# S5 + pooling + short-convolution trunk: ScalarE empties the small PSUM tiles of the S5 input part, and the recurrence's VectorE operations are spread one by one

## Chip, cores and metric

One core of a Trainium2 chip. The metric is the device time of one launch in microseconds (us). The kernel before took 1664.32 us as the median of three runs (1661.87 to 1665.4).

## What is computed

A trunk of two layers on x of 1 x 1024 x 1024 in float32. The part that matters here is branch A of the first layer, a diagonal complex state-space mixer (S5) with 64 groups of 16 channels and 64 complex states each:

```python
h = rmsnorm(h_res, norm_g[layer])
u_a, g_a, u_b, g_b = split(h @ ev_w_in, 4)
# s5_mixer, per group g:
dt = exp(log_dt);  lb = exp(lam * dt)            # complex
bb = ((lb - 1) / lam) * b                        # complex
bu = einsum('blgh,gph->blgp', u_a, bb)
s  = associative_scan(s[t] = lb * s[t-1] + bu[t])
y  = real(einsum('blgp,ghp->blgh', s, c)) + d_skip * u_a
y  = gelu(y);  z = y @ w_glu + b_glu;  y_a = val * sigmoid(gate)
# branch B: causal pooling over windows 2, 4, 8, 16, then small matmuls
h_res += concat([y_a * silu(g_a), y_b * silu(g_b)]) @ ev_w_out
```

The second layer (short gated convolution) and a last rmsnorm follow.

## The kernel before

**Matmuls.** Every large product is a list of units, run in order on TensorE (PE). A unit of `mm_full` is 8 blocks over the contraction dimension (k-blocks); each is six matmuls of 128x512 (weights split into `whi` + `wlo`, activations into `a` + `t`, three products, two column halves; L114). The accumulators `acc` are a ring of 3 PSUM tiles. The units are: 0 to 7 "ua" (input of S5), 8 and 9 "ga" 0 and 1 (gate of S5), 10 to 29 four groups of "ub", "ub", "gb", "gb", "pool" (branch B), 30 to 35 "ga" 2 to 7, 36 to 43 "fb" (output projection of B), then the GLU, "fa", the second layer and its output. For each unit its weights are split (ScalarE makes `whi`, L81; VectorE `wlo`, L82), and `evac_*` empties `acc` (a VectorE operation 128x1024 first).

**The written order.** All engines take their instructions in program order. Work that isn't a unit's own stands in three tables by unit: `pre`, `post`, and `mids`. `mm_full` puts a unit's list of `mids` into the seven gaps between its k-blocks (`spread`). The small matmuls among them write `aux`, a ring of 2 PSUM tiles: a third small product waits until the first tile has been emptied.

**S5 input part (units 6 to 9).** POOL (GpSimd) prepares tables (`s5_tables`, to about 85 us), then for each k of 0 to 7 a tile Z(k) (`z_build`: a product on VectorE or POOL, 128x896, and further products and sums on POOL). `t_work(k)`: three pieces; each multiplies Z(k) by identity columns and by C1 (L390) into `aux`; from there 128 columns per group go to the tile M (ScalarE, L391) and 16 to the tile K (VectorE adds them to what is in K, a diagonal of skip weights that POOL put there). `x_work(k)`: two pieces; M times the layer's input U (L408) into `aux`, and from there to W (tile name `big`): the first 64 partitions by ScalarE (L416), the others by VectorE (L414).

```python
        o = [lambda k=k: s5_step(k // 2 - 1, True)] if k in (2, 4, 6) else []
        at_mid(s, [t[0], x[0], t[1], x[1], *n, t[2], *b, *o])
    at_mid(9, [*x_work(7), lambda: s5_step(3, True)])
    for i, m in enumerate((("gb", 7), ("ga", 2), ("ga", 3), ("ga", 4))):
        at_mid(idx[m], [lambda i=i: s5_step(i, False)])
```

**Recurrence.** The states stand in W as 128 chunk values (NC) for each of 32 pairs of groups. `s5_step(i, odd)` adds to the odd (or even) columns of one quarter of W the products of their left neighbours with lambda: four VectorE operations on 128x1024 (even: 128x1008), product, add, product, add, with the scratch tile `t9`. Between the odd and the even steps `s5_scan` on POOL runs over the odd columns (63 rounds of four small operations, after unit 9). `s5_kd` stores K in DRAM through a zeroed tile in `t9` (ahead of unit 10).

**Output of the state part.** `y_prep(k)` (POOL, ScalarE) prepares, and the two pieces of `y_work(k)` (units ga3 to ga6 and fb1 to fb4) multiply into `aux` (L485, L486) and apply gelu in five operations: ScalarE square (L487), VectorE multiply-add (L236), VectorE product with `aux` (L230), ScalarE tanh (L490), VectorE sum and product (L491), which is the last to read `aux`.

**Ahead of unit 0's end.** ScalarE computes sines for the tables (L299 to L301, behind POOL), then loads another function table and takes the square root for the first rmsnorm (L154); VectorE makes `rs` from it and PE spreads `rs` over the partitions (L168).

Of the kernel before, what the change touches and what calls it, by code (L numbers as in the profile page):

```python
# [8 lines left out]
F32 = mybir.dt.float32  # L9
# [5 lines left out]
P = 128  # L15
# [3 lines left out]
NG = 64  # L19
# [8 lines left out]
def trunk(ctx: ExitStack, tc: tile.TileContext, a: dict, out: bass.AP):  # L28
# [177 lines left out]
    limW = cp.tile([P, 2, 32], F32, name="limW")  # L206
    lre2 = cp.tile([P, 32], F32, name="lre2")
    lim2 = cp.tile([P, 2, 32], F32, name="lim2")
    st1 = cp.tile([P, 2, 32], F32, name="st1")
    st2 = cp.tile([P, 2, 32], F32, name="st2")  # L210
    fri = cp.tile([P, 2, NG], F32, name="fri")

    s5 = {}
# [15 lines left out]
    def tt(e, o, x, y, op):  # L229
        e.tensor_tensor(out=o, in0=x, in1=y, op=op)  # L230
# [48 lines left out]
    def s5_tables():  # L279
# [45 lines left out]
        for i in range(2):  # L325
# [3 lines left out]
            e.tensor_copy(cols_of(limW[p0, 1]), by[p0, 1, :, i])  # L329

        tt(e, lre2, lreW, lreW, ALU.mult)
        tt(e, st1[:, 0], limW[:, 0], limW[:, 0], ALU.mult)
        tt(e, lre2, lre2, st1[:, 0], ALU.subtract)
        both = lambda x: x.unsqueeze(1).to_broadcast([P, 2, 32])
        tt(e, lim2, limW, both(lreW), ALU.mult)
        ts(e, lim2, lim2, 2.0, ALU.mult)

        s5["K"] = slot("K", [P, NG, NH])
        tt(e, s5["K"], mask.unsqueeze(1).to_broadcast([P, NG, NH]),
           w[:, 3].unsqueeze(2).to_broadcast([P, NG, NH]), ALU.mult)  # L340
        ts(e, s5["C1"], s5["C1"], sgn[:, 0:1], ALU.mult)

    def s5_b():
        P1, P2 = s5["P1"], s5["P2"]
# [36 lines left out]
    def t_work(k):  # L381

        def piece(g0, g1):
            if g0 == 0:
                s5["M", k] = slot(("t1", "t6")[k % 2], [P, 8, P])
            n = g1 - g0
            ps = aux_tile()
            v = ps[:, : IW * n].rearrange("p (g x) -> p g x", x=IW)
            for g in range(g0, g1):
                PE.matmul(v[:, g - g0], lhsT=s5["Z", k][:, g], rhs=s5["IC"][k % 2][:, g], start=True, stop=True)  # L390
            A.activation(s5["M", k][:, g0:g1], v[:, :, 0:P], AF.Copy)  # L391
            kk = s5["K"][:, 8 * k + g0 : 8 * k + g1]
            tt(V, kk, kk, v[:, :, P:], ALU.add)

        return [lambda: piece(0, 3), lambda: piece(3, 6), lambda: piece(6, 8)]

# [5 lines left out]
    def x_work(k):  # L402
        def piece(q):
            W, U = s5["W"], s5["U"][k]
            ps = aux_tile()
            for i in range(4):
                g = 4 * q + i
                PE.matmul(ps[:, i * P : i * P + P], lhsT=s5["M", k][:, g], rhs=U[:, g], start=True, stop=True)  # L408
            p0 = slice(64 * (k % 2), 64 * (k % 2) + 64)
            g0 = (k // 2) * 8 + 4 * q  # L410
            for ri in range(2):
                o = W[p0, ri, g0 : g0 + 4].rearrange("p a b -> p (a b)")
                if ri:
                    V.tensor_copy(o, ps[64:128])  # L414
                else:
                    A.activation(o, ps[0:64], AF.Copy)  # L416

        return [lambda: piece(0), lambda: piece(1)]

# [9 lines left out]

    def s5_step(i, odd):  # L430

        W, gs = s5["W"], slice(8 * i, 8 * i + 8)
        n = NC // 2 if odd else NC // 2 - 1
        src = W[:, :, gs, 0:NC:2] if odd else W[:, :, gs, 1 : NC - 1 : 2]
        dst = W[:, :, gs, 1:NC:2] if odd else W[:, :, gs, 2:NC:2]
        t = slot("t9", [P, 2, 8, NC // 2])[:, :, :, 0:n]
        sh = [P, 2, 8, n]
        re, im = lreW[:, gs].unsqueeze(1).unsqueeze(3).to_broadcast(sh), limW[:, :, gs].unsqueeze(3).to_broadcast(sh)
        for x, f in ((src, re), (src[:, ::-1], im)):
            tt(V, t, x, f, ALU.mult)  # L440
            tt(V, dst, dst, t, ALU.add)

    def s5_scan():
        W = s5["W"]
        re = lre2.unsqueeze(1).to_broadcast([P, 2, 32])
        for c in range(3, NC, 2):
            tt(G, st1, W[:, :, :, c - 2], re, ALU.mult)
            tt(G, st2, W[:, ::-1, :, c - 2], lim2, ALU.mult)
# [26 lines left out]
    def y_work(k):  # L475
        def piece(q):
# [577 lines left out]
    for k in range(8):  # L1054
# [2 lines left out]
        t, x = t_work(k), x_work(k - 1) if k else [lambda: None] * 2  # L1057
        b = [lambda k=k: z_build(k + 2)] if k < 6 else []
        n = [lambda k=k: u_load(k + 1, UT[(k + 1) % 2])] if k < 7 else []
        o = [lambda k=k: s5_step(k // 2 - 1, True)] if k in (2, 4, 6) else []  # L1060
        at_mid(s, [t[0], x[0], t[1], x[1], *n, t[2], *b, *o])
    at_mid(9, [*x_work(7), lambda: s5_step(3, True)])
    for i, m in enumerate((("gb", 7), ("ga", 2), ("ga", 3), ("ga", 4))):
        at_mid(idx[m], [lambda i=i: s5_step(i, False)])
    at(pre, 10, s5_kd)
    at(post, 9, s5_scan)

    def c2_load():
        s5["C2"] = slot("C2", [P, NG, NH])
# [391 lines left out]
```

## Time and profile before

| | |
|---|---|
| median of three runs | 1664.32 us (1661.87 to 1665.4) |
| the profiled execution | 1662.76 us, its span in the trace 1661.0 us |
| busy: PE / VectorE (DVE) / ScalarE (ACT) / GpSimd (POOL) | 96% / 67% / 32% / 40% of the span |
| mean granted TensorE clock | 0.978 |

Times of the trace are counted from the span's start. PE is the engine that sets the end; a gap on it, or a stretch in which its clock was granted at half, is time lost.

### The profile page before, as it was taken

Reading aid. Unit: us, or ns where it says so; the run is one execution under the profiler, and the core shown is the slowest. Engines: PE = TensorE matmul, PEld = TensorE weight load, DVE = VectorE, ACT = ScalarE, POOL = GpSimd, SP = SyncE. Lnnn points to the kernel's source line nnn. Section 1 sums busy time; section 2 is a strip of 40 time slices with the busy share of each in tenths; the row PEclk is TensorE's granted clock in tenths of the full one; section 3 lists DMA queues with packets and bytes.
Section 4 is the critical chain, followed back from the end, with each engine's and each line's share of the span. In section 5 each row is a group of like instructions: output and inputs, shape, how many; then the busy total and the mean of one; then the engine's idle time right before and its main releaser. Section 6 shows DMA issues by size and latency. Waiting matters only on the chain.

```text
span 1661.0 us, 19044 instructions
## 1 busy us (share of the span) xinstructions
PE 1594.5 (96%) x7186; PEld 1318.9 (79%) x7186; DVE 1107.8 (67%) x1302; ACT 537.7 (32%) x777; POOL 664.4 (40%) x638
## 2 busy tenths in 40 slices
PE   9987999999799999999969999999999999999997
PEld 8776888888688878888747888888888888878886
DVE  5546646679765686672599776868686877763544
ACT  6132211112353343341433332323333233343531
POOL 6962399806312443201264534535343435300001
PEclk9998999999899999999989999999999999999998
DMA  5232362123486722224402212221221212156353
GB/s 210 102 102 76 85 174 91 50 70 127 139 292 201 255 90 76 77 79 149 151 1 76 77 51 76 66 87 52 76 77 57 96 51 77 55 199 207 123 149 117
DMA packets 95034, 181.29 MB, mean 109 GB/s; under 512 B 16352, under 2 KB 52960, under 8 KB 94432
## 3 DMA queue, kind: packets, MB, share of 16 engines
q10 hardware_dynamic: 49664, 116.41, 21.7%
q1 hardware_dynamic: 45280, 63.68, 11.4%
q8 instruction: 57, 0.93, 0.2%
q14 instruction: 33, 0.27, 0.1%
HBM read 141.33 MB, written 42.93 MB: 111 GB/s over the span
## 4 chain that ended last, share of the span: by engine, by line
PE 58%; DVE 5%; issue 1%; DMA 1%; ACT 0%; ACTq 0%; DVEq 0%
PE acc L682 43%; PE acc L929 9%; PE acc L114 4%; PE acc L833 1%; DVE t L230 1%; DVE a L82 1%; DVE a L85 1%; DVE ws L82 1%; PE acc L972 1%; DMA t<-in_glu 0%; DMA hpd<-t 0%; PE aux L168 0%; DVE big L82 0%; ACTq L907 0%; PE aux L150 0%
## 5 line engine op out<-in xcount | busy, mean ns | idle before, releaser
L682 PE MATMUL acc<-a,ws 128*128 128x512 f32 x1920 | 450.5, 390 | 5.5 <-DVE t L230 2.4
L682 PEld LDWEIGHTS acc<-a,ws 128*128 128x128 f32 x1920 | 361.1, 188 | 82.9 <-ACT a L81 3.8
L114 PE MATMUL acc<-a,whi 128*128 128x512 f32 x1440 | 396.6, 398 | 0.1
L114 PEld LDWEIGHTS acc<-a,whi 128*128 128x128 f32 x1440 | 271.5, 191 | 55.7 <-issue 0.9
L230 POOL TENSOR_TENSOR t<-t,t 128x512 f32<-128x512 f32 (+2 forms) x81 | 147.7, 1823 | 308.4 <-DVE ws L82 183.7
L682 PE MATMUL acc<-big,ws 128*128 128x512 f32 x960 | 230.1, 395 | 11.5 <-DVE big L82 4.1
L82 DVE TENSOR_TENSOR wlo<-raw,whi 128x1024 fp32r<-128x1024 f32 (+2 forms) x89 | 114.5, 1289 | 188.3 <-ACT whi L81 188.1
L81 ACT ACTIVATE ws<-t 128x512 fp32r<-128x512 f32 x200 | 125.8, 630 | 338.1 <-PE acc L682 205.5
L682 PEld LDWEIGHTS acc<-big,ws 128*128 128x128 f32 x960 | 182.1, 190 | 53.1 <-DVE big L82 5.4
L114 PE MATMUL acc<-a,wlo 128*128 128x512 f32 x720 | 223.9, 392 | 0.0
L82 DVE TENSOR_TENSOR ws<-t,ws 128x512 fp32r<-128x512 f32 x200 | 182.5, 913 | 33.4 <-ACT ws L81 31.6
L114 PEld LDWEIGHTS acc<-a,wlo 128*128 128x128 f32 x720 | 136.7, 190 | 29.0
L929 PE MATMUL acc<-a,whi 128*128 128x512 f32 x480 | 150.3, 394 | 1.5 <-ACT a L84 1.1
L81 ACT ACTIVATE whi<-raw 128x1024 fp32r<-128x1024 f32 (+2 forms) x89 | 86.8, 978 | 198.1 <-PE acc L114 128.4
L230 DVE TENSOR_TENSOR t<-t,acc 128x512 f32<-128x512 f32 x134 | 91.1, 681 | 50.6 <-PE acc L682 50.5
L682 PE MATMUL acc<-td,ws 128*128 128x512 f32 x480 | 117.3, 393 | 1.3 <-DVE td L82 1.3
L682 PEld LDWEIGHTS acc<-td,ws 128*128 128x128 f32 x480 | 90.6, 189 | 21.9 <-DVE td L82 1.7
L929 PEld LDWEIGHTS acc<-a,whi 128*128 128x128 f32 x480 | 90.7, 189 | 21.7 <-ACT a L84 1.5
L230 POOL TENSOR_TENSOR t<-C,LR 128x1024 f32<-128x1024 f32 (+1 forms) x18 | 40.1, 2231 | 160.5 <-PE aux L486 70.7
L929 PE MATMUL acc<-a,wlo 128*128 128x512 f32 x240 | 94.3, 393 | 0.0
L230 POOL TENSOR_TENSOR t<-t,rs 128x512 f32<-128x512 f32 x5 | 8.7, 1746 | 198.4 <-ACT rs L169 198.4
L230 POOL TENSOR_TENSOR raw<-raw,raw 128x512 f32<-128x512 f32 x20 | 26.7, 1336 | 120.6 <-DVE ws L82 120.6
(259 smaller groups left out, 1986.8 us busy)
## 6 DMA issues: line engine op xcount, KB each, us to landing
raw<-in_scin ACTq DMA_DIRECT2D x32, 512.0 KB, 4.1
t<-in_scin ACTq DMA_DIRECT2D x32, 512.0 KB, 4.3
raw<-in_scout ACTq DMA_DIRECT2D x32, 512.0 KB, 3.7
raw<-in_win ACTq DMA_DIRECT2D x29, 512.0 KB, 3.6
t<-ud ACTq DMA_DIRECT2D x16, 512.0 KB, 4.0
raw<-in_wout ACTq DMA_DIRECT2D x16, 512.0 KB, 3.7
big<-y2d ACTq DMA_DIRECT2D x15, 512.0 KB, 6.1
ud<-t SPq DMA_DIRECT2D x8, 512.0 KB, 2.6
```

The costliest lines, as they stand in the source:

```text
L81: A.activation(h, src, AF.Copy)
L82: (e or V).tensor_tensor(out=l, in0=src, in1=h, op=ALU.subtract)
L85: V.scalar_tensor_tensor(out=l, in0=src, scalar=scale, in1=h, op0=ALU.mult, op1=ALU.subtract)
L114: PE.matmul(acc[:, n * 512 : n * 512 + 512], lhsT=w, rhs=x[:, n * 512 : n * 512 + 512], start=first and i == 0, stop=last and i == 2)
L230: e.tensor_tensor(out=o, in0=x, in1=y, op=op)
L682: PE.matmul(bank, lhsT=wt, rhs=x[:, k], start=k == 0 and j == 0, stop=k == 3 and j == 2)
L833: PE.matmul(u.acc[:, hs], lhsT=w, rhs=x[:, hs], start=k == 0 and j == 0, stop=k == NK - 1 and j == 2)
L929: PE.matmul(acc[:, 0:512], lhsT=w, rhs=x[:, n % 2], start=n == 0 and i == 0, stop=n == 15 and i == 2)
L972: PE.matmul(acc, lhsT=wt, rhs=x[:, n % 2, quarter(q)], start=n == 0 and i == 0, stop=n == 15 and i == 2)
```

## The change

- `t_work`: K gets its 16 columns by a ScalarE copy, no longer by a VectorE add. POOL no longer fills K with the skip diagonal; instead the new `s5_skip`, after unit 9, makes the diagonal in `t9` and adds it to K (two VectorE operations on 128x1024).
- The sign that C1 is multiplied by (128x1024) is applied by ScalarE, no longer by POOL.
- `x_work`: both halves of W by ScalarE.
- `s5_step` returns its four operations singly; the odd ones stand between the pieces of `t_work` and `x_work`, over two k's, the last odd step moves to unit 10. The even steps stand one unit earlier each (gb6, gb7, ga2, ga3), spread singly. `s5_scan` moves behind unit 10.
- gelu: the square takes its factor as the ScalarE operation's scale; one VectorE operation (`(w + 1) * aux`) stands for two.
- Scratch tiles st1, st2 are replaced by other scratch.

```diff
         tt(e, lre2, lreW, lreW, ALU.mult)
-        tt(e, st1[:, 0], limW[:, 0], limW[:, 0], ALU.mult)
-        tt(e, lre2, lre2, st1[:, 0], ALU.subtract)
+        tt(e, tm[:, 0:32], limW[:, 0], limW[:, 0], ALU.mult)
+        tt(e, lre2, lre2, tm[:, 0:32], ALU.subtract)
...
-        tt(e, s5["K"], mask.unsqueeze(1).to_broadcast([P, NG, NH]),
-           w[:, 3].unsqueeze(2).to_broadcast([P, NG, NH]), ALU.mult)
-        ts(e, s5["C1"], s5["C1"], sgn[:, 0:1], ALU.mult)
+        V.tensor_copy(skip, w[:, 3])
+        A.activation(s5["C1"], s5["C1"], AF.Copy, scale=sgn[:, 0:1])
+
+    def s5_skip():
+
+        t = slot("t9", [P, NG, NH])
+        tt(V, t, mask.unsqueeze(1).to_broadcast([P, NG, NH]), skip.unsqueeze(2).to_broadcast([P, NG, NH]), ALU.mult)
+        tt(V, s5["K"], s5["K"], t, ALU.add)
...
             A.activation(s5["M", k][:, g0:g1], v[:, :, 0:P], AF.Copy)
-            kk = s5["K"][:, 8 * k + g0 : 8 * k + g1]
-            tt(V, kk, kk, v[:, :, P:], ALU.add)
+            A.activation(s5["K"][:, 8 * k + g0 : 8 * k + g1], v[:, :, P:], AF.Copy)
...
-                if ri:
-                    V.tensor_copy(o, ps[64:128])
-                else:
-                    A.activation(o, ps[0:64], AF.Copy)
+                A.activation(o, ps[64 * ri : 64 * ri + 64], AF.Copy)
...
-        for x, f in ((src, re), (src[:, ::-1], im)):
-            tt(V, t, x, f, ALU.mult)
-            tt(V, dst, dst, t, ALU.add)
+        def product(x, f, first):
+            if first:
+                tmp["t"] = slot("t9", [P, 2, 8, NC // 2])[:, :, :, 0:n]
+            tt(V, tmp["t"], x, f, ALU.mult)
+
+        take = lambda: tt(V, dst, dst, tmp["t"], ALU.add)
+        return [lambda: product(src, re, True), take, lambda: product(src[:, ::-1], im, False), take]
...
-            A.activation(w, ps, AF.Square)
-            ts(V, w, w, 0.044715, ALU.mult, 1.0, ALU.add)
-            tt(V, w, w, ps, ALU.mult)
+            A.activation(w, ps, AF.Square, scale=math.sqrt(0.044715))
+            V.scalar_tensor_tensor(out=w, in0=w, scalar=1.0, in1=ps, op0=ALU.add, op1=ALU.mult)
...
-        o = [lambda k=k: s5_step(k // 2 - 1, True)] if k in (2, 4, 6) else []
-        at_mid(s, [t[0], x[0], t[1], x[1], *n, t[2], *b, *o])
-    at_mid(9, [*x_work(7), lambda: s5_step(3, True)])
-    for i, m in enumerate((("gb", 7), ("ga", 2), ("ga", 3), ("ga", 4))):
-        at_mid(idx[m], [lambda i=i: s5_step(i, False)])
+        if k % 2 == 0:
+            o = [lambda k=k, i=i: odd_work[k // 2 - 1][i]() for i in range(4)] if k else [lambda: None] * 4
+            at_mid(s, [t[0], x[0], t[1], x[1], *n, o[0], t[2], *b])
+        else:
+            at_mid(s, [t[0], o[1], x[0], t[1], o[2], x[1], *n, t[2], o[3], *b])
+    at_mid(9, x_work(7))
+    at_mid(10, [lambda i=i: odd_work[3][i]() for i in range(4)])
+    for i, m in enumerate((("gb", 6), ("gb", 7), ("ga", 2), ("ga", 3))):
+        at_mid(idx[m], [lambda i=i, j=j: even_work[i][j]() for j in range(4)])
+    at(post, 9, s5_skip)
     at(pre, 10, s5_kd)
-    at(post, 9, s5_scan)
+    at(post, 10, s5_scan)
```

Where the instructions stand. In these rows `big` is W, `t<-B,LR` a product of `z_build`, and numbers behind a name tell buffers apart.

First place: VectorE in unit 7, before. The first row empties `aux` of the last t piece of k = 2.

```order
L230 TENSOR_TENSOR K_409<-K_409,aux_979 128x32
L230 TENSOR_TENSOR t_98_990<-B_50_657,LR_142 128x128x7
L230 TENSOR_TENSOR t_100_997<-big_804,lreW 128x1024
L230 TENSOR_TENSOR big_804<-big_804,t_100_997 128x2x512
L230 TENSOR_TENSOR t_100_997<-big_804,limW 128x1024
L230 TENSOR_TENSOR big_804<-big_804,t_100_997 128x2x512
L230 TENSOR_TENSOR K_409<-K_409,aux_1009 128x48
L414 COPY big_804<-aux_1015 64x512
L230 TENSOR_TENSOR K_409<-K_409,aux_1028 128x48
```

All four operations of the odd step stand together, and behind them the K add and the W copy of the pieces of k = 3. After the change, VectorE in the same unit:

```order
L229 TENSOR_TENSOR t_97_978<-big_803,lreW 128x1024
L229 TENSOR_TENSOR t_99_991<-B_50_656,LR_143 128x128x7
L229 TENSOR_TENSOR big_803<-big_803,t_97_978 128x2x512
L229 TENSOR_TENSOR t_97_978<-big_803,limW 128x1024
L229 TENSOR_TENSOR big_803<-big_803,t_97_978 128x2x512
L229 TENSOR_TENSOR t_108_1053<-B_50_656,LR_143 128x128x7
L82 TENSOR_TENSOR wlo_1067<-raw_925,whi_1066 128x1024
```

The VectorE has no operation on `aux` left there, and its next split of weights stands behind the step. What empties `aux` is ScalarE; its rows in the second half of unit 7 after the change (`aux_999` and `aux_1019` are t pieces of k = 3, `aux_1012` and `aux_1032` x pieces; x2: both halves):

```order
L394 ACTIVATE t_101_998<-aux_999 128x384
L395 ACTIVATE K_408<-aux_999 128x48
L415 ACTIVATE big_803<-aux_1012 64x512 x2
L394 ACTIVATE t_101_998<-aux_1019 128x384
L395 ACTIVATE K_408<-aux_1019 128x48
L415 ACTIVATE big_803<-aux_1032 64x512 x2
```

The copy of `aux_1012` writes W behind the step's first add, that of `aux_1032` behind its second product (both by data).

Second place: VectorE from unit gb6 to the last pool unit, before. The first row is branch B's split of its pooled input, the `acc` rows are evacuations, L516 the gate's product; `acc_2771` is unit gb7's.

```order
L82 TENSOR_TENSOR td_265_2630<-t_274_2705,td_264_2629 128x1024
L82 TENSOR_TENSOR wlo_2761<-raw_2686,whi_2760 128x512
L230 TENSOR_TENSOR t_278_2766<-acc_2711,rs_290 128x1024
L516 SCALAR_TENSOR_TENSOR t_278_2766<-t_279_2767,t_278_2766 128x1024
L230 TENSOR_TENSOR t_281_2814<-big_804,lreW 128x16x63
L230 TENSOR_TENSOR big_804<-big_804,t_281_2814 128x2x8x63
L230 TENSOR_TENSOR t_281_2814<-big_804,limW 128x16x63
L230 TENSOR_TENSOR big_804<-big_804,t_281_2814 128x2x8x63
L82 TENSOR_TENSOR wlo_2826<-raw_2764,whi_2825 128x1024
L230 TENSOR_TENSOR t_284_2831<-acc_2771,rs_290 128x1024
L516 SCALAR_TENSOR_TENSOR t_284_2831<-t_285_2832,t_284_2831 128x1024
L82 TENSOR_TENSOR wlo_2863<-raw_2829,whi_2862 128x1024
```

After the change (the first row is the last operation of the even step that now stands in gb6; L520 is the same gate product, `acc_2778` gb7's accumulator):

```order
L229 TENSOR_TENSOR big_803<-big_803,t_277_2726 128x2x8x63
L82 TENSOR_TENSOR wlo_2768<-raw_2688,whi_2767 128x512
L229 TENSOR_TENSOR t_280_2773<-acc_2713,rs_289 128x1024
L520 SCALAR_TENSOR_TENSOR t_280_2773<-t_281_2774,t_280_2773 128x1024
L229 TENSOR_TENSOR t_283_2791<-big_803,lreW 128x16x63
L229 TENSOR_TENSOR big_803<-big_803,t_283_2791 128x2x8x63
L229 TENSOR_TENSOR t_283_2791<-big_803,limW 128x16x63
L229 TENSOR_TENSOR big_803<-big_803,t_283_2791 128x2x8x63
L82 TENSOR_TENSOR wlo_2833<-raw_2771,whi_2832 128x1024
L229 TENSOR_TENSOR t_286_2838<-acc_2778,rs_289 128x1024
L520 SCALAR_TENSOR_TENSOR t_286_2838<-t_287_2839,t_286_2838 128x1024
L82 TENSOR_TENSOR wlo_2870<-raw_2836,whi_2869 128x1024
```

One even step (rows of 128x1008 elements) more stands ahead of the `wlo` that unit ga2 multiplies with and of the operation that empties gb7's accumulator.

Third place: ScalarE between the sines and the square root of the first rmsnorm, before.

```order
L300 ACTIVATE td_11_185<-td_11_185 128x64
L301 ACTIVATE td_11_185<-td_11_185,half_pi 128x64
L154 ACT_TABLE_LOAD
L154 ACTIVATE rsm<-rsm 128x8
L81 ACTIVATE whi_549<-raw_281 128x1024
```

After the change:

```order
L299 ACTIVATE td_11_184<-td_11_184 128x64
L300 ACTIVATE td_11_184<-td_11_184,half_pi 128x64
L338 ACTIVATE C_14_204<-C_14_204,sgn 128x1024
L154 ACT_TABLE_LOAD
L154 ACTIVATE rsm<-rsm 128x8
L81 ACTIVATE whi_548<-raw_280 128x1024
```

The multiplication of C1 by its sign stands between the last sine and the table load for the square root.

## Rows read from the trace of the kernel before

**Rows 1.** Waits of PE from 80 to 190 us: total, times, longest.

```profile
PE aux L390 <- DVE K L230: 12.9, 6, 4.0
```

**Rows 2.** Timeline, PE: start, us, instruction [idle before, and its releaser].

```profile
44.42 3.59 PE L168 MATMUL aux<-rs,ones 128*128 128x512 f32 x4 [2.46 <-DVE rs L230]
...
90.61 1.81 PE L390 MATMUL aux<-td,t 128*128 128x144 f32 x6 [4.47 <-POOL t L230]
...
126.91 1.81 PE L390 MATMUL aux<-td,t 128*128 128x144 f32 x6 [4.04 <-DVE K L230]
...
153.27 1.59 PE L390 MATMUL aux<-td,t 128*128 128x144 f32 x6 [4.02 <-DVE K L230]
...
167.24 1.81 PE L390 MATMUL aux<-td,t 128*128 128x144 f32 x6 [2.75 <-DVE K L230]
...
382.38 1.07 PE L114 MATMUL acc<-a,whi 128*128 128x512 f32 x4
...
383.74 1.07 PE L114 MATMUL acc<-a,whi 128*128 128x512 f32 x4
...
418.59 0.46 PE L485 MATMUL aux<-t,td 128*128 128x128 f32 x2 [3.88 <-issue]
...
438.74 0.77 PE L485 MATMUL aux<-t,td 128*128 128x128 f32 x2 [5.15 <-DVE B L491]
```

**Rows 3.** Stretches: PE, PEld, DVE, ACT, POOL busy (x count), PE clock, DMA share, GB/s.

```profile
89.00:96.00 7.00, 5.39 (x19) 4.82 (x20) 1.10 (x2) 0.49 (x1) 6.89 (x4) 0.54 0.42 164
...
126.00:133.00 7.00, 6.09 (x21) 5.52 (x22) 2.44 (x5) 1.67 (x3) 0.00 (x0) 0.52 0.14 40
...
153.00:157.00 4.00, 3.73 (x16) 3.58 (x17) 1.11 (x4) 1.41 (x3) 0.00 (x0) 0.57 0.00 0
...
436.00:444.00 8.00, 5.26 (x21) 4.95 (x22) 5.91 (x9) 2.83 (x5) 0.00 (x0) 0.57 0.23 66
```

**Rows 4.** Timeline, POOL: end of the tables, and the first operation after the scan.

```profile
81.03 1.94 POOL L230 TENSOR_TENSOR K<-con,td 128x1024 f32<-128x1024 f32 x1
...
82.95 2.86 POOL L234 TENSOR_SCALAR C<-C,sgn 128x1024 f32<-128x1024 f32 x1
...
387.01 2.73 POOL L230 TENSOR_TENSOR t<-C,LR 128x1024 f32<-128x1024 f32 x1 [59.82 <-DVE t L581]
```

**Rows 5.** Timeline, DVE, unit 7.

```profile
119.92 2.87 DVE L230 TENSOR_TENSOR big<-big,t 128x1024 f32<-128x1024 f32 x1
...
122.83 2.64 DVE L230 TENSOR_TENSOR t<-big,limW 128x1024 f32<-128x1024 f32 x1
...
126.65 0.20 DVE L230 TENSOR_TENSOR K<-K,aux 128x48 f32<-128x48 f32 x1
```

**Rows 6.** Lines by shape, 80 to 190 us: busy, mean ns, idle before and releasers.

```profile
L414 DVE COPY big<-aux 64x512 f32<-64x512 f32 x16 | 11.1, 694 | 16.8 <-ACT big L416 16.7
...
L416 ACT ACTIVATE big<-aux 64x512 f32<-64x512 f32 x16 | 9.4, 590 | 27.0 <-DVE big L230 14.2 <-PE aux L408 12.8
```

**Rows 7.** Timeline, ACT: an operation of 128x1024 with a column as scale.

```profile
19.85 1.14 ACT L1265 ACTIVATE a<-big,vec 128x1024 fp32r<-128x1024 f32 x1
```

**Rows 8.** Timeline, DVE, units gb7 to ga4.

```profile
372.93 1.20 DVE L230 TENSOR_TENSOR t<-big,lreW 128x1008 f32<-128x1008 f32 x1
...
377.78 1.23 DVE L82 TENSOR_TENSOR wlo<-raw,whi 128x1024 fp32r<-128x1024 f32 x1
...
378.93 1.22 DVE L230 TENSOR_TENSOR t<-acc,rs 128x1024 f32<-128x1024 f32 x1
...
383.22 1.23 DVE L82 TENSOR_TENSOR wlo<-raw,whi 128x1024 fp32r<-128x1024 f32 x1 [0.66 <-ACT whi L81]
...
403.29 1.91 DVE L230 TENSOR_TENSOR t<-big,lreW 128x1008 f32<-128x1008 f32 x1
...
414.17 2.14 DVE L236 TENSOR_SCALAR K<-K 128x512 f32<-128x512 f32 x1
...
417.80 0.69 DVE L491 SCALAR_TENSOR_TENSOR B<-K,aux 128x512 f32<-128x512 f32 x1 [0.70 <-ACT K L490]
```

More of the change, by code (lines that the diff above doesn't have):

```diff
@@ L200, in trunk @@
     rsm = cp.tile([P, 3, 8], F32, name="rsm")
+    skip = cp.tile([P, NG], F32, name="skip")
     psch = cp.tile([P, 8], F32, name="psch")
@@ L208, in trunk @@
     lim2 = cp.tile([P, 2, 32], F32, name="lim2")
-    st1 = cp.tile([P, 2, 32], F32, name="st1")
-    st2 = cp.tile([P, 2, 32], F32, name="st2")
     fri = cp.tile([P, 2, NG], F32, name="fri")
@@ L435, in s5_step @@
         dst = W[:, :, gs, 1:NC:2] if odd else W[:, :, gs, 2:NC:2]
-        t = slot("t9", [P, 2, 8, NC // 2])[:, :, :, 0:n]
-        sh = [P, 2, 8, n]
+        sh, tmp = [P, 2, 8, n], {}
         re, im = lreW[:, gs].unsqueeze(1).unsqueeze(3).to_broadcast(sh), limW[:, :, gs].unsqueeze(3).to_broadcast(sh)
-        for x, f in ((src, re), (src[:, ::-1], im)):
-            tt(V, t, x, f, ALU.mult)
-            tt(V, dst, dst, t, ALU.add)
+        def product(x, f, first):
[4 more added lines that the diff above has]
+        return [lambda: product(src, re, True), take, lambda: product(src[:, ::-1], im, False), take]
     def s5_scan():
@@ L445, in s5_scan @@
         re = lre2.unsqueeze(1).to_broadcast([P, 2, 32])
+        st1, st2 = (fri[:, i].rearrange("p (r g) -> p r g", r=2) for i in range(2))
         for c in range(3, NC, 2):
@@ L1042, in trunk @@
     s5["U"] = {}
+    odd_work, even_work = [], []
     def w_alloc():
         s5["W"] = slot("big", [P, 2, 32, NC])
+        odd_work.extend(s5_step(i, True) for i in range(4))
+        even_work.extend(s5_step(i, False) for i in range(4))
     def at_mid(s, work):
```

## Prediction

> **What bounds the kernel now.** I read the timeline of TensorE first, for its gaps, since it is busy 96% of the span: what it waits for inside 80 to 450 us is what the change can give back. In the S5 input part it waits six times for the VectorE's K add, 12.9 us in all [rows 1]; the three large ones are 4.04 us at 126.91, 4.02 at 153.27 and 2.75 at 167.24, so the other three make 2.1. Ahead of these it waits 4.47 us at 90.61 for POOL, and in the output part 3.88 us at 418.59 and 5.15 at 438.74 [rows 2]. The releaser of 418.59 is given as "issue", but the tile that this product needs is freed by the gelu's last operation, 417.80 + 0.69 = 418.49 [rows 8], so it is a VectorE wait too.
>
> Then the stretches behind these gaps: the granted clock averages 0.54, 0.52 and 0.57 in them, which is about the lower of the two levels (1.2 of 2.4 GHz), and it fell after a gap of 4 us or more in each case [rows 3]. What a stretch loses is its PE time by (1 - clock): 5.39 x 0.46 = 2.5 us after 90.61, 6.09 x 0.48 = 2.9 after 126.91, 3.73 x 0.43 = 1.6 after 153.27, 5.26 x 0.43 = 2.3 after 438.74.
>
> Last the VectorE's rows, to see why K is late: the odd step's four operations stand in one block. Two of them take 2.87 and 2.64 us, and only then, at 126.65, comes the K add of 0.20 us that TensorE waits for [rows 5].
>
> **First t piece (gain 7.0).** POOL drops the K product (1.94) and the C1 scaling (2.86) that stand just ahead of Z(0) [rows 4]. TensorE's wait ends at 90.61 on a POOL product; moved up by 4.80 us it would come at 85.8, and TensorE arrives at 90.61 - 4.47 = 86.1. So the wait goes, and I count its slow clock as gone too: 4.5 + 2.5. Bounds: 0 if something else is late there (7.0 lost), and no more than 7.0.
>
> **C1 on ScalarE (loss 1.1).** The operation stands between the sines and the table load that precedes the first square root, whose result TensorE waits for at 44.42 (2.46 us) [rows 2]. A ScalarE operation of 128x1024 with a column as scale took 1.14 us [rows 7], and the whole of it is on that chain. Bounds 0 and 1.14 plus a slower stretch; the clock is already low there.
>
> **K and W copies, odd steps (gain 10.4 + 4.5).** After the change nothing of VectorE frees `aux` in units 6 to 9; ScalarE does. The price of a W copy is 590 ns on ScalarE against 694 on VectorE [rows 6]. So two copies in series, 1.18, are no longer than one of each, 1.28. The K copy (128x48 or 128x32) has no row on ScalarE; it lies between nothing and the 0.59 of ten times its columns, and I take 0.2, as the VectorE's add [rows 5].
>
> The Trainium skill, "ScalarE: Activation LUTs", Rules for kernel authors, speaks against such a move: simple elementwise work belongs on VectorE, up to about three times as fast per element in bf16. If that held here, a pair of copies would end some 3 us later and the gaps would stay, about 15 us of the sum. The rows above say the contrary for fp32 out of PSUM.
>
> What ScalarE waits for now is data: the x copy that follows an odd step's first add must wait for that add. In unit 7 the add ran from 119.92 to 122.8 [rows 5]. It now has the Z product between it and the step's first product, which has moved ahead of the piece by which Z is paced; so it may start some 1.2 us earlier, and 0.4 more as the small wait before is gone: about 118.3, end 121.2 if it is as long as before. Two copies take it to 122.4; TensorE comes for the tile at 126.91 - 4.04 - 0.4 = 122.5. That is no margin, but no wait to speak of: I count both 4 us gaps, the three small ones and the slow stretches of 2.9 and 1.6 us as gone. Bounds: 0 to 1.5 us left in each of units 7 and 8.
>
> In unit 9 the wait of 2.75 us stays but for 0.3: ScalarE reaches its M and K copies only behind the tanh of the gate unit 8, which waits for the VectorE's split and evacuation as before. Bounds of its gain: 0 and 2.75 with its slow stretch of 1.6.
>
> So 12.9 - 2.75 + 0.3 = 10.4, and 2.9 + 1.6 = 4.5.
>
> **Last odd step, skip and scan (0).** The step in unit 10 has to wait for the DMA of `s5_kd` that reads the zeroed `t9`, and the scan starts after it, up to 20 us later than before. POOL was idle for 59.82 us ahead of 387.01, so it ended at 327.2 [rows 4]; the even steps need it at 369, so 20 us are covered. If the scan came 42 us later, every further one would be TensorE's. Behind the waiting step on VectorE stands the weight split of two units later: covered unless the DMA takes over 15 us.
>
> **Even steps one unit earlier, gelu (gain 4.0).** VectorE has no free time from gb6 on. A step takes 377.78 - 372.93 = 4.85 us there. One more of them now stands ahead of the `wlo` (377.78) and of the evacuation of gb7's accumulator (378.93, 1.22 us) [rows 8]. The evacuation ends at 378.93 + 4.85 + 1.22 = 385.0. Unit ga2 takes that accumulator at 382.38 [rows 2]: a new wait of 2.6 us. All VectorE work behind it is 4.85 late, less the 0.66 us that it idled at 383.22, so 4.2. The first gelu piece ended at 418.49; it now has one operation less (2.14 us at 414.17) [rows 8], so it ends at 418.5 + 4.2 - 2.1 = 420.6. TensorE waits for it as before, 2.0 us later, and the product stands one k-block (383.74 - 382.38 = 1.36 us) earlier in its unit, with that much left to do: 3.4 lost in all, the ga2 wait inside it, as TensorE is early there. But no step stands in ga4 any more (it ran for 10.9 us in front of the first gelu, 403.29 to 414.17, as one does before 438.74), so the wait there goes: 5.15 + 2.3 - 3.4 = 4.0. The other gelu operations saved lie where VectorE isn't waited for. Bounds: -3.4 (438.74 stays) to 7.4 (nothing new).
>
> **Sum.** 7.0 - 1.1 + 10.4 + 4.5 + 4.0 = 24.8 us. On the profiled execution 1662.76 - 24.8 = 1638.0; the median shown is 1.6 above that execution, so I predict 1639.
>
> **The rivals.**
>
> *ScalarE is held by the steps.* If POOL's Z operations run beside all four operations of an odd step, as in the step from 403.29 to 414.17, which takes 10.9 us instead of 4.85 [rows 8], the adds end 1 to 1.6 us later than I have them, and the x copies, with the M and K copies behind them on ScalarE, free the tiles late: 1.5 us at two or three places in units 7 and 8, with a slow stretch in each: 3 to 9 us. Time 1642 to 1648. For it: no margin in my schedule, and the add and the product in unit 7 already took 2.87 and 2.64. The Trainium skill, "GPSIMD Engine Reference", Specifications, says that GpSimd's SBUF interfaces are shared with VectorE, with contention for VectorE operations with two SBUF inputs. By that rule all four would be slowed whenever POOL works; the trace agrees, as the same shape takes 1.2 us without POOL.
>
> *The VectorE's queue at gb6 to ga3.* The extra 4.85 us costs a slow stretch after the ga2 wait (1.6, as after 153.27) that isn't absorbed, and one more wait at ga5: the 4.0 are lost, with 1 to 3 more. Time 1643 to 1646.
>
> *The gaps only change hands.* Units 7 and 8 wait for ScalarE's copies as long as for VectorE's: 8.1 + 4.5 stay. Time 1652. Against it: the K copies no longer stand behind the block.
>
> *Slower than before.* In units 7 to 9 ScalarE holds everything that frees `aux`, so one late add delays three pieces, not one. Nine pieces late by 3 us each, with a slow clock behind five of them (some 2 us each, as above), cost 27 + 10 = 37 us on top of the forecast, whose units 7 and 8 have no gaps: 1638 + 37 = 1675. It decides where the pieces are late by 1.7 us each, since 9 x 1.7 + 10 is the forecast's 25. Against it: VectorE has several short operations less per unit there.
>
> **Chances.** The forecast, 1633 to 1644: 0.66. ScalarE held: 0.13. VectorE's queue: 0.10. Gaps change hands: 0.04. Better than forecast, by a unit 9 wait that goes and a first root without loss (1628 to 1633): 0.03. Slower: 0.02, and as much for a time within 0.2% of before, which is about what a measurement of this kernel can tell from no change. Faster by more than that: 0.96. The range of 8 in 10 takes the first three: 1631 to 1649.
>
> **What would show it.** Right: no wait at 86, 122 and 149 us, the wait at 44 longer by 1.1, one of 2 to 3 us in unit 9, a new one of about 2.6 at ga2, one of 3 to 5 at ga4, none at ga5. Wrong: waits of L393 on ScalarE's W copies in units 7 and 8, or VectorE waits at ga5 to ga6.

## The result, and the profile after

The changed kernel takes 1636.09 us (median of four runs, 1634.49 to 1639.64) against 1663.87 us before (the three runs shown ahead and a fourth): ratio 0.9837, 95% interval 0.9817 to 0.9857, so 27.8 us less. Forecast were 1639, range 1631 to 1649. The profiled execution took 1635.34 us with a span of 1633.5.

Waits of PE after the change (total, times, longest). Of the six waits for K [rows 1] and the two in the output part, one each is left, the last and the first of these lines; the other two, for unit gb7's accumulator at ga2 (2.6) and for a load (1.5), are new:

```profile
PE aux L490 <- issue: 4.1, 1, 4.1
...
PE acc L114 <- DVE t L229: 2.6, 1, 2.6
...
PE aux L490 <- DMA td<-md: 1.5, 1, 1.5
...
PE aux L393 <- ACT K L395: 1.5, 1, 1.5
```

Where they lie, in PE's timeline after (start, us, instruction, [idle before and releaser]), in answer to [rows 2]:

```profile
46.76 3.65 PE L168 MATMUL aux<-rs,ones 128*128 128x512 f32 x4 [5.01 <-DVE rs L229]
...
88.35 0.90 PE L393 MATMUL aux<-td,t 128*128 128x144 f32 x6
...
116.01 0.90 PE L393 MATMUL aux<-td,t 128*128 128x144 f32 x6
...
134.56 0.90 PE L393 MATMUL aux<-td,t 128*128 128x144 f32 x6
...
146.85 1.00 PE L393 MATMUL aux<-td,t 128*128 128x144 f32 x6 [1.47 <-ACT K L395]
...
361.99 1.17 PE L114 MATMUL acc<-a,whi 128*128 128x512 f32 x4 [2.58 <-DVE t L229]
...
397.22 0.46 PE L490 MATMUL aux<-t,td 128*128 128x128 f32 x2 [4.15 <-issue]
...
415.12 0.46 PE L490 MATMUL aux<-t,td 128*128 128x128 f32 x2 [1.54 <-DMA td<-md]
```

There is no idle time ahead of the first t product (88.35), and none ahead of the second t products of k = 3 (116.01) and k = 5 (134.56), the places of the 4.04 and 4.02 us before. PE runs there at full clock, where it ran at about half of it behind these gaps [rows 3]; two stretches (the clock stands behind the five engines' busy times):

```profile
89.00:96.00 7.00, 7.00 (x41) 6.11 (x40) 3.90 (x3) 2.71 (x10) 4.67 (x3) 1.00 0.48 165
...
126.00:133.00 7.00, 7.00 (x44) 6.23 (x43) 3.90 (x4) 3.83 (x12) 1.97 (x2) 1.00 0.46 152
```

A slow stretch stays in the output part: behind the 4.15 us at 397.22 the granted clock averages 0.66 from 397 to 402 us.

To say where the time came from, I cut the span of both traces at instructions that both have: the first rms product (L168), the first and last t product (L390, after: L393), the first and last output product (L486, after: L491) and the last input matmul (L114). Each number is the difference of two starts in one trace, in us; differences named below are taken before rounding:

| | to first rms | to first t | t part | to first output | output part | to last L114 | rest | span |
|---|---|---|---|---|---|---|---|---|
| before | 44.4 | 46.2 | 91.2 | 218.4 | 142.7 | 257.2 | 860.9 | 1661.0 |
| after | 46.8 | 41.6 | 70.4 | 222.7 | 135.6 | 256.9 | 859.7 | 1633.5 |

The t part and the piece ahead of it give 25.5 us, the output part with what leads to it 2.9; the start loses 2.3 (46.76 against 44.42).

### The profile page after: what moved, and what is told of

Read it like the earlier page. It is cut to its first block, busy times and chain, and to the rows that moved or that the text cites. A ratio compares the mean times of both kernels' runs of the same rounds, so it can differ in the third digit from the quotient of the medians.

```text
span 1633.5 us, 19047 instructions
## 1 busy us (share of the span) xinstructions
PE 1581.8 (97%) x7186; PEld 1308.3 (80%) x7186; DVE 1074.0 (66%) x1249; ACT 550.4 (34%) x818; POOL 661.3 (40%) x636
## 3 DMA queue, kind: packets, MB, share of 16 engines
q1 hardware_dynamic: 45280, 63.68, 11.6%
## 4 chain that ended last, share of the span: by engine, by line
PE 59%; DVE 5%; issue 1%; DMA 1%; ACT 0%; ACTq 0%; DVEq 0%
PE acc L686 44%; PE acc L933 9%; PE acc L114 4%; PE acc L837 1%; DVE t L229 1%; DVE a L85 1%; DVE ws L82 1%; PE acc L976 1%; DVE a L82 0%; DMA t<-in_glu 0%; DMA hpd<-t 0%; PE aux L168 0%; DVE big L82 0%; ACTq L911 0%; PE aux L150 0%
## 5 line engine op out<-in xcount | busy, mean ns | idle before, releaser
L114 PE MATMUL acc<-a,whi 128*128 128x512 f32 x1440 | 393.3, 395 | 3.3 <-DVE t L229 2.6
L114 PEld LDWEIGHTS acc<-a,whi 128*128 128x128 f32 x1440 | 268.3, 189 | 58.9 <-issue 4.0
L686 PE MATMUL acc<-big,ws 128*128 128x512 f32 x960 | 230.9, 396 | 11.6 <-DVE ws L82 4.7
L114 PE MATMUL acc<-a,wlo 128*128 128x512 f32 x720 | 222.6, 390 | 0.0
L114 PEld LDWEIGHTS acc<-a,wlo 128*128 128x128 f32 x720 | 136.0, 189 | 28.8
L686 PEld LDWEIGHTS acc<-td,ws 128*128 128x128 f32 x480 | 91.2, 190 | 21.2 <-issue 1.3
L933 PEld LDWEIGHTS acc<-a,whi 128*128 128x128 f32 x480 | 90.0, 188 | 21.6 <-ACT a L84 1.5
L229 POOL TENSOR_TENSOR t<-C,LR 128x1024 f32<-128x1024 f32 (+1 forms) x18 | 42.6, 2372 | 141.3 <-PE aux L491 62.3
```

What stands on the lines that cost most here:

```text
L114: PE.matmul(acc[:, n * 512 : n * 512 + 512], lhsT=w, rhs=x[:, n * 512 : n * 512 + 512], start=first and i == 0, stop=last and i == 2)
L686: PE.matmul(bank, lhsT=wt, rhs=x[:, k], start=k == 0 and j == 0, stop=k == 3 and j == 2)
L933: PE.matmul(acc[:, 0:512], lhsT=w, rhs=x[:, n % 2], start=n == 0 and i == 0, stop=n == 15 and i == 2)
```

## Experiments

All start from the changed kernel and undo or move one part. Each ratio is to runs of the kernel before that were made beside that experiment (their medians lie from 1663.2 to 1664.6 us). The same cut of each one's trace:

| | median | ratio to before, interval | to first t | t part | to first output + output part |
|---|---|---|---|---|---|
| changed kernel | 1636.1 | 0.9837, 0.9817 to 0.9857 | 41.6 | 70.4 | 358.2 |
| e1_block | 1651.1 | 0.9921, 0.9902 to 0.9940 | 42.2 | 83.5 | 358.1 |
| e2_kdve | 1640.1 | 0.9855, 0.9840 to 0.9869 | 41.3 | 73.1 | 358.9 |
| e9_wdve | 1642.2 | 0.9870, 0.9855 to 0.9884 | 42.6 | 74.1 | 359.8 |
| e6_pool_tables | 1643.9 | 0.9882, 0.9868 to 0.9895 | 46.1 | 73.2 | 359.1 |
| e4_c1_late | 1636.7 | 0.9832, 0.9818 to 0.9847 | 41.4 | 70.4 | 358.6 |
| e3_even_old | 1635.7 | 0.9828, 0.9811 to 0.9846 | 42.9 | 70.4 | 358.1 |
| e5_gelu_old | 1641.6 | 0.9869, 0.9855 to 0.9882 | 42.2 | 70.4 | 362.8 |
| e8_y_old | 1639.9 | 0.9858, 0.9844 to 0.9872 | 41.5 | 70.4 | 360.4 |
| e10_even_late | 1628.1 | 0.9779, 0.9763 to 0.9795 | 42.1 | 70.4 | 349.5 |
| e7_combined | 1625.0 | 0.9766, 0.9753 to 0.9779 | 42.8 | 70.4 | 347.5 |

One trace is one execution. The changed kernel, e1, e2, e4, e6 and e9 have the same code in the output part, and the last column differs among them by 1.8 us (358.1 to 359.8), so a difference of less than that in it says nothing by itself.

**The odd steps in a block again (e1_block).**

```diff
-        if k % 2 == 0:
-            o = [lambda k=k, i=i: odd_work[k // 2 - 1][i]() for i in range(4)] if k else [lambda: None] * 4
-            at_mid(s, [t[0], x[0], t[1], x[1], *n, o[0], t[2], *b])
-        else:
-            at_mid(s, [t[0], o[1], x[0], t[1], o[2], x[1], *n, t[2], o[3], *b])
+        o = [lambda k=k: [f() for f in odd_work[k // 2 - 1]]] if k in (2, 4, 6) else []
+        at_mid(s, [t[0], x[0], t[1], x[1], *n, t[2], *b, *o])
```

> The changed kernel, but the four operations of each odd step stand in one block behind the third t piece again (units 7 and 8), as before the change; ScalarE alone still empties the small PSUM tiles. Theory (what counts is the spreading): the K copy no longer stands behind the block, but the x copies into W must wait for the whole block by data, so the gap moves from the second t product to the second x product, releaser ScalarE's W copy, about 4 to 5.5 us in each of units 7 and 8 with a slow stretch of about 2 us behind each: 1636 + 12 to 15 = 1648 to 1651 us. Rival (moving K and W copies to ScalarE is what removed the gaps): at most 3 us over the changed kernel, 1636 to 1639 us, no gap over 1.5 us in units 7 and 8.

1651.1 us. The gaps are back, one product further on, and now for ScalarE's W copy (PE's timeline, then ScalarE's, where the copy waits for the block's last operation):

```profile
122.12 1.94 PE L410 MATMUL aux<-t,t 128*128 128x128 f32 x8 [4.03 <-ACT big L415]
...
146.54 2.07 PE L410 MATMUL aux<-t,t 128*128 128x128 f32 x8 [4.03 <-ACT big L415]
```

```profile
115.18 0.49 ACT L394 ACTIVATE t<-aux 128x384 f32<-128x384 f32 x1 [2.59 <-PE aux L393]
...
115.57 0.20 ACT L395 ACTIVATE K<-aux 128x48 f32<-128x48 f32 x1
...
120.87 1.20 ACT L415 ACTIVATE big<-aux 64x512 f32<-64x512 f32 x2 [5.09 <-DVE big L229]
```

M and K of the t piece go out at once (115.18, 115.57), so the ring's other tile is what holds PE. That is the theory's case; the move to ScalarE alone doesn't remove the gaps. Of the 13.2 us that the t part is longer, 1.6 aren't the block's: in unit 9 this execution has the same wait as the changed kernel (1.46 us), but the clock fell behind it (its rows stand in the last section).

**K by VectorE, or half of W by VectorE (e2_kdve, e9_wdve).**

```diff
-            A.activation(s5["K"][:, 8 * k + g0 : 8 * k + g1], v[:, :, P:], AF.Copy)
+            V.tensor_copy(s5["K"][:, 8 * k + g0 : 8 * k + g1], v[:, :, P:])      # e2_kdve
...
-                A.activation(o, ps[64 * ri : 64 * ri + 64], AF.Copy)
+                if ri:
+                    V.tensor_copy(o, ps[64:128])                                 # e9_wdve
+                else:
+                    A.activation(o, ps[0:64], AF.Copy)
```

> The changed kernel, but K gets its columns from PSUM by a VectorE copy instead of a ScalarE copy; W copies stay on ScalarE and the odd steps stay spread. Theory (spreading counts): a K copy now stands behind single step operations of at most 2.9 us; waits of 0.5 to 1.5 us at one or two places in each of units 7 to 9, 1636 + 1 to 4 = 1637 to 1640 us; in unit 9 the K copy stands behind the gate's product again, about 1 us more there. Rival (ScalarE for K is the cure): gaps of about 3 to 4 us in units 7 and 8 with slow stretches, 1646 us or more.

> The changed kernel, but the second half of each W copy goes by VectorE again, as before the change; K copies stay on ScalarE and the odd steps stay spread. Theory (the spreading is what counts, and a copy that takes its place among single step operations is late by one of them at most): 0 to 2 us over the changed kernel, 1636 to 1638 us, no gap over 1.5 us in units 7 and 8. Rival (a VectorE copy in the ring of two small PSUM tiles is held behind the steps whichever way they stand): gaps of 2 to 4 us with slow stretches in units 7 and 8, 1642 us or more.

1640.1 and 1642.2 us; in the t part they cost 2.8 and 3.7. PE's timeline of e2_kdve, and of e9_wdve:

```profile
107.23 1.00 PE L393 MATMUL aux<-td,t 128*128 128x144 f32 x6 [0.39 <-DVE K L395]
...
147.02 1.43 PE L393 MATMUL aux<-td,t 128*128 128x144 f32 x6 [2.14 <-ACT big L415]
```

```profile
129.19 1.05 PE L410 MATMUL aux<-t,t 128*128 128x128 f32 x7 [0.47 <-DVE big L416]
...
149.40 1.00 PE L393 MATMUL aux<-td,t 128*128 128x144 f32 x6 [2.15 <-ACT K L395]
...
151.09 2.02 PE L410 MATMUL aux<-t,t 128*128 128x128 f32 x8 [0.68 <-ACT K L395]
```

In units 7 and 8 each of the two has a single gap, under half a us; the rest is unit 9, where the first wait grows by 0.7 and a slow stretch follows (its first product takes 1.43 us in e2_kdve, its second 2.02 in e9_wdve, against 1.00 and 1.16 after the change). So e2_kdve fell on the theory's side, though by its row the wait in unit 9 ended with ScalarE's W copy and not, as I had expected, with K. e9_wdve has the rival's time and the theory's gaps: of its 6.1 us in the median, its trace puts 3.7 into the t part, nearly all in unit 9, which I had left out, and 1.0 ahead of it and 1.6 into the output part with what leads to it, where its edit does nothing. No run has the steps spread and both copies on VectorE, so what the move to ScalarE gives as a whole isn't shown; each half alone is worth 2.8 and 3.7 us in these traces.

**POOL's work and C1 (e6_pool_tables, e4_c1_late).**

```diff
         V.tensor_copy(skip, w[:, 3])
-        A.activation(s5["C1"], s5["C1"], AF.Copy, scale=sgn[:, 0:1])
+        tt(G, s5["K"], mask.unsqueeze(1).to_broadcast([P, NG, NH]),     # e6_pool_tables
+           w[:, 3].unsqueeze(2).to_broadcast([P, NG, NH]), ALU.mult)
+        ts(G, s5["C1"], s5["C1"], sgn[:, 0:1], ALU.mult)          # e6_pool_tables
...
     def s5_b():
         P1, P2 = s5["P1"], s5["P2"]
+        A.activation(s5["C1"], s5["C1"], AF.Copy, scale=sgn[:, 0:1])    # e4_c1_late
```

> The changed kernel, but POOL makes the skip diagonal in K (it is overwritten later, so this is work added) and scales C1 again, both just ahead of the first Z product, and ScalarE does not scale C1. Theory: a wait of about 4.5 us ahead of the first t product and a slow stretch of 2.4 us behind it come back, the first rms is 1 us earlier: 1636 + 4.5 + 2.4 - 1.0 = 1642 us. Rival (something else is late there, or the gap is caught up later by a shorter wait): 1636 to 1638 us.

> The changed kernel, but ScalarE's scaling of C1 stands some 20 us later, where ScalarE is idle, instead of ahead of the first square root. Theory: the wait ahead of the first rms product is 1.05 us shorter, all of which reaches the end: 1635 us. Rival: start-up transfers set that wait and the operation was hidden: no difference in the gap between the last sine and the square root's end beyond the operation itself, the wait ahead of the rms product as long as after the change, 1636 us.

e6_pool_tables: 1643.9 us, 7.8 over the changed kernel where 6 had been expected; the wait is back, 4.00 us against 4.47, with a slow stretch (PE's timeline: the next four matmuls take 2.08 us; 4.5 us more to the first t product and 2.9 in the t part):

```profile
92.21 1.81 PE L395 MATMUL aux<-td,t 128*128 128x144 f32 x6 [4.00 <-POOL t L229]
...
93.64 2.08 PE L114 MATMUL acc<-a,whi 128*128 128x512 f32 x4
```

e4_c1_late: 1636.7 us, no difference that the medians can tell. On ScalarE the term is exact, though. After the change:

```profile
40.93 0.26 ACT L298 ACTIVATE td<-td 128x64 f32<-128x64 f32 x1 [7.30 <-POOL td L235]
...
41.62 1.13 ACT L338 ACTIVATE C<-C,sgn 128x1024 f32<-128x1024 f32 x1
...
44.07 0.21 ACT L154 ACTIVATE rsm<-rsm 128x8 f32<-128x8 f32 x1
```

From the first sine to the square root it takes 44.07 - 40.93 = 3.14 us with the C1 operation (1.13) and 2.10 in the trace before and in e4_c1_late, so 1.04. But the first sine itself starts anywhere from 39.53 (before) to 41.57 us (e7_combined) in these traces, as the POOL chain ahead of it starts when the transfer of its input lands (10.43 to 11.46 us): 1 us here is less than what a start differs by.

**Output part (e3_even_old, e5_gelu_old, e8_y_old).** Even steps as before, gelu as before, both:

```diff
-    for i, m in enumerate((("gb", 6), ("gb", 7), ("ga", 2), ("ga", 3))):
-        at_mid(idx[m], [lambda i=i, j=j: even_work[i][j]() for j in range(4)])
+    for i, m in enumerate((("gb", 7), ("ga", 2), ("ga", 3), ("ga", 4))):      # e3, e8
+        at_mid(idx[m], [lambda i=i: [f() for f in even_work[i]]])
...
-            A.activation(w, ps, AF.Square, scale=math.sqrt(0.044715))
-            V.scalar_tensor_tensor(out=w, in0=w, scalar=1.0, in1=ps, op0=ALU.add, op1=ALU.mult)
+            A.activation(w, ps, AF.Square)                                    # e5, e8
+            ts(V, w, w, 0.044715, ALU.mult, 1.0, ALU.add)
+            tt(V, w, w, ps, ALU.mult)
```

> The changed kernel, but the four even steps stand in units gb7, ga2, ga3 and ga4 again, in blocks. Theory: the 2.6 us wait ahead of ga2 and the 1.5 us wait for a transfer at ga5 go, a wait of about 4.5 us with a slow stretch of 2.3 us ahead of ga5's first output piece comes back: 3 to 4 us slower, 1639 to 1640 us. Rival (the moved steps cost VectorE's queue as much as they give): 1635 to 1637 us.

> The changed kernel with the gelu of before (three VectorE operations instead of two). Theory (the gelu's operation is on the path at the first output pieces, where VectorE is late): the wait ahead of ga4's piece is 2.1 us longer, about 6.3 us instead of 4.15, the others stay: 1638 us. Rival (gelu is hidden): 1636 us, the wait as in the changed kernel.

> The changed kernel with the even steps at their old places, in blocks, and the gelu of before: the output part as before, the rest changed. Theory (of the two only the gelu gives anything; the steps' move alone gave nothing): waits of about 3.9 us at ga4 and 5.2 us at ga5 with slow stretches as before the change, 2 to 3 us over the changed kernel, 1638 to 1639 us. Rival (the step's move is worth the predicted 4 us where the gelu is long): 1640 us or more.

1635.7, 1641.6 and 1639.9 us. PE's timeline in the output part of e3_even_old, then of e5_gelu_old:

```profile
393.66 0.46 PE L490 MATMUL aux<-t,td 128*128 128x128 f32 x2 [1.62 <-issue]
...
412.78 0.77 PE L490 MATMUL aux<-t,td 128*128 128x128 f32 x2 [5.76 <-DVE B L495]
```

```profile
362.88 2.05 PE L114 MATMUL acc<-a,whi 128*128 128x512 f32 x4 [2.57 <-DVE t L229]
...
400.36 0.77 PE L490 MATMUL aux<-t,td 128*128 128x128 f32 x2 [5.06 <-issue]
...
418.94 0.46 PE L490 MATMUL aux<-t,td 128*128 128x128 f32 x2 [2.44 <-DMA td<-md]
```

With the steps at their old places the waits at ga2 and for the transfer go, the one at ga4 shrinks to 1.62 us, and 5.76 us at ga5 come: with one of 0.30 further on 7.7 us of waits against 2.58 + 4.15 + 1.54 = 8.3 after the change, and the same 358 us in all. So the rival was right: the steps' move gave nothing that can be told.

The long gelu costs 4.6 us with the moved steps, twice what I had expected, and 360.4 - 358.1 = 2.3 with the old ones. Of the 4.6, 2.2 are there at ga4's product and 0.7 more at ga5's, since the transfer comes later still. The last 1.6 come behind ga5's wait of 2.44 us, where the clock fell (0.67 from 419 to 423 us; 1.00 at that place after the change). They aren't the gelu's: e9_wdve, with the output code of the changed kernel, has such a stretch there, too, and is 1.6 longer by it. The slow stretch behind ga2's wait (362.88) costs nothing: in e1_block and e9_wdve, which have it, the first output piece comes as late after the last t product as after the change (238.5 us), and PE only waits less for it. e8_y_old lies between its two forecasts (to 1639, and from 1640). Of the two edits only the gelu gained (medians 1639.9 against 1635.7 with the steps at their old places), and its size is known only to within the 1.8 us above.

**A version that goes further (e10_even_late, e7_combined).** An even step is needed only by the pieces of its own quarter of W, so the third and fourth have time until fb1 and fb3:

```diff
-    for i, m in enumerate((("gb", 6), ("gb", 7), ("ga", 2), ("ga", 3))):
+    for i, m in enumerate((("gb", 7), ("ga", 2))):
...
         at_mid(ysteps[k], y_work(k))
+        if k in (2, 3):
+            at_mid(ysteps[k], [lambda k=k, j=j: even_work[k][j]() for j in range(4)])
...
-            at(pre, ysteps[k] - 1, lambda k=k: mi_load(k // 2))
+            at(pre, ysteps[k] - (2 if k == 2 else 1), lambda k=k: mi_load(k // 2))   # e7 alone
```

e7_combined has the C1 operation late, too.

> The combined version without its other two parts: the changed kernel with even steps in gb7, ga2 and, behind the output pieces, ga5 and ga6; C1 scaling and the load of M where the changed kernel has them. Theory (the places of the last two even steps carry the gain): waits at ga2 and ga4 gone, the wait for the load of M at ga5 still there with up to 3 us: 1627 to 1630 us. Rival (the load of M or C1 carries a good part): 1631 us or more.

> A version of the changed kernel: C1 scaled by ScalarE some 20 us later; even steps in gb7, ga2 and then, behind the output pieces, in ga5 and ga6 (the pieces that need them come later still); the load of M for the third output piece one unit earlier on its queue. Theory: the waits at ga2 (2.6), ga4 (4.1) and ga5 (1.5) all go, as no even step stands between the first two output pieces and their gelu, and the rms is 1 us earlier: 1636 - 8 - 1 = 1627 us, less up to 1.5 for slow stretches. Rival (VectorE's lack of time only moves on): a new wait of 3 us or more at ga6 to fb1, 1631 us or more.

1628.1 and 1625.0 us. In e10_even_late one wait is left in the output part, for the load of M:

```profile
403.88 0.46 PE L490 MATMUL aux<-t,td 128*128 128x128 f32 x2 [1.70 <-DMA td<-md]
```

In e7_combined there is none. Its stretches, where PE is busy throughout (columns as above):

```profile
340.00:395.00 55.00, 55.00 (x269) 46.42 (x268) 43.33 (x37) 19.12 (x21) 25.47 (x10) 1.00 0.47 148
...
395.00:410.00 15.00, 15.00 (x92) 13.32 (x91) 8.10 (x8) 6.55 (x8) 9.19 (x5) 1.00 0.55 156
...
420.00:450.00 30.00, 30.00 (x143) 25.11 (x142) 26.01 (x24) 14.41 (x16) 6.27 (x3) 1.00 0.80 266
```

It is 2.3% faster than the kernel before, and its interval lies below that of the changed kernel.

## Why the prediction was right, point by point

**First t piece: 7.0 forecast.** 4.6 us to the first t product; the slow stretch of 2.5 behind it is in the t part's sum. Undone by itself, 4.5 and 2.9 come back. Right.

**C1: 1.1 lost.** 1.04. The start of the trace lost 2.3 us, the rest of it because the first sine came 1.40 us later (40.93 against 39.53): its input landed 0.64 later (11.07 against 10.43), and POOL's chain from there, where the change edits nothing, took 29.9 us instead of 29.1 (29.1 to 30.1 in the twelve traces). The sign that I had named, a wait of PE at 44 us longer by 1.1, says nothing: it is 5.01 us instead of 2.46, but 2.47 to 7.95 in the experiments.

**K and W copies, odd steps: 10.4 + 4.5.** With the 2.5 above, 17.4 were forecast for the t part and 91.23 - 70.35 = 20.9 came. The gaps of 4.04 and 4.02 are gone with their slow stretches, as forecast, by the spreading above all (undone: 13.2 us of the t part, 11.6 without unit 9). The copies cost what the forecast has, a W copy 593 ns on ScalarE and a K copy 0.2 us. The margin in units 7 and 8, which I had put at nothing, is wide, so the gaps' going didn't hang on luck: VectorE after the change in unit 7, then ScalarE in unit 7 (first row) and unit 9:

```profile
113.32 1.22 DVE L229 TENSOR_TENSOR big<-big,t 128x1024 f32<-128x1024 f32 x1
...
116.83 2.30 DVE L229 TENSOR_TENSOR t<-big,limW 128x1024 f32<-128x1024 f32 x1 [2.30 <-ACT big L415]
```

```profile
116.21 1.21 ACT L415 ACTIVATE big<-aux 64x512 f32<-64x512 f32 x2 [1.62 <-PE aux L410]
...
146.22 0.47 ACT L394 ACTIVATE t<-aux 128x384 f32<-128x384 f32 x1
...
146.59 0.20 ACT L395 ACTIVATE K<-aux 128x48 f32<-128x48 f32 x1
```

The step's first add ends at 113.32 + 1.22 = 114.5 (I had let it take 2.87), while the W copy that depends on it starts at 116.21, after idling for PE alone. What was too small is first unit 9: 0.3 forecast, 2.4 came. M goes at 146.22 behind the gate's tanh and K right behind it, at 146.59, where K before had to wait for the gate's product on VectorE, so PE waits 1.47 + 0.21 instead of 2.75, which gives 1.1. I had also kept the slow stretch, and it didn't come after this shorter gap: from there to the third t piece PE took 171.97 - 167.24 = 4.73 us before and 150.44 - 146.85 - 0.21 = 3.38 after. That part is partly luck, since in e1_block it did come behind the same gap. The other 1.4 us of the 3.5 lie in PE's busy time about the gaps that went. Some 0.2 us a gap is my estimate for this: a gap also ends the overlap of neighbouring matmuls (after the change, the first t product starts 0.45 us after a pair that takes 0.62). The rest isn't traced.

**Last odd step, skip, scan: 0.** Right: VectorE idled 5.64 us for the transfer in unit 10, and POOL's scan, ending at 318 us with the operation behind it, was 27 us ahead of the first even step (345.70).

**Even steps and gelu: 4.0.** 361.1 - 358.2 = 2.9 came, but the step of the prediction that gave the credit was wrong. The new waits were sized right (ga2 2.58 against 2.6, ga4 4.15 against 3 to 5), and the wait at 438.74 did go. What failed is "no step stands in ga4 any more, so the wait there goes" as the reason for a gain: the moved steps cost as much as they give (358.1 us with the steps at their old places, 358.2 with the new). With the gelu of before they seem to lose 362.8 - 360.4 = 2.4, but 1.6 of that is the slow stretch that e9_wdve has, too, so a loss isn't shown. The one operation less in the gelu is most of what came, 2.2 of 2.9 (360.4 - 358.2). So this term had nearly the right size by luck. I had also left out a wait: the load of M for ga5's piece stands on SP's queue behind eight stores of the first output piece, which stand behind a store that waits for VectorE (SP's timeline after the change):

```profile
384.34 20.11 SPq L529 DMA_DIRECT2D sgad<-t  x2
...
404.50 4.45 SPq L503 DMA_DIRECT2D yd<-B  x8
...
408.99 0.44 SPq L477 DMA_DIRECT2D td<-md  x1
```

PE waits 1.54 us for its landing at 415.12.

**The rest** differs by 1.2 us. Over the twelve traces it lies between 859.7 and 861.9 with no order in it, so this isn't the change.

**The sum.** Its terms give 1638.0 + 1.6 = 1639.6, which the forecast has as 1639. The total came within 3 us because the errors are small and of both signs: 3.5 too little in the t part, 1.1 too much in the output part, 1.2 too little lost at the start, and some 1.5 that drifted in the rest.

**The rivals.** ScalarE held by the steps: no; only with the block does it wait (e1_block). VectorE's queue at gb6 to ga3: half right, as above; the wait at ga5 came, but for a load. Gaps that change hands: not with the steps spread, but just that without (e1_block). Slower: no.

## What to carry to other kernels

Where a ring of small PSUM tiles is emptied by an engine that also has long work, spread that work singly before moving the emptying: the move alone left the gap in place under another engine's name. Place a producer by when its own consumer comes, not by when it could run: the even steps that came one unit earlier cost what they gave, and putting the last two later, behind the output pieces, gave 8 us. When two edits touch one stretch, undo each alone; the sum of the two had the right size and the wrong owner.

## What the runs showed of the hardware

As these rows read, VectorE and POOL don't slow each other by a share: where both operands of the VectorE operation lie in SBUF, one holds the other off. POOL's rows after the change in unit 7, to be read beside VectorE's above:

```profile
113.57 2.77 POOL L229 TENSOR_TENSOR t<-t,t 128x896 f32<-128x896 f32 x1 [5.03 <-DVE t L229]
...
116.31 1.74 POOL L229 TENSOR_TENSOR t<-B,LR 128x896 f32<-128x896 f32 x1
```

VectorE's add started first (113.32) and took its usual 1.22; POOL's sum, started 0.25 us later, took 2.77 instead of the 1.95 to 1.97 of six of the eight of its kind. VectorE's product started at 116.83, during a POOL product that ended at 116.31 + 1.74 = 118.05, and ended at 116.83 + 2.30 = 119.13, 1.08 us after it. The add of [rows 5] ended at 119.92 + 2.87 = 122.79, 1.08 us after a POOL sum that ran from 118.93 for 2.78. In the even step in ga2 after the change, too, three operations started beside a POOL operation end 1.06 to 1.07 us after it. So, by these rows, who starts first decides. That the two share their way to SBUF is what the Trainium skill, "GPSIMD Engine Reference", Specifications, says; the trace agrees.

The length of a gap of PE did not settle whether its clock fell. Behind the gap of 1.47 us in unit 9 the granted clock stayed at 1.00 in the changed kernel, and behind the same gap it fell in e1_block (0.69 from 158 to 163 us; the second row is four matmuls, 1.17 us at full clock):

```profile
158.25 1.00 PE L393 MATMUL aux<-td,t 128*128 128x144 f32 x6 [1.46 <-ACT K L395]
...
160.88 2.05 PE L114 MATMUL acc<-a,whi 128*128 128x512 f32 x4
```

After the same gap of 2.58 us at ga2 it fell in some executions (2.04 and 2.05 us for the next four matmuls in e1_block, e5_gelu_old and e9_wdve) and not in others (1.17 after the change). Of all gaps over 1 us from 80 to 545 us in the twelve traces, those of 1.3 to 1.9 us had a lower mean clock in the 4 us behind them in 1 case of 16, those of 2.1 to 3.2 us in 8 of 15, and those of 3.9 us and more in all 16 (0.50 to 0.65 there).
